# Attention weights of the third token group turned in 32 by 32 blocks on VectorE, with SBUF transfers on ScalarE's queue

## The chip, the cores and the metric

The kernel runs on 1 core of one Trainium2 chip. The metric is device time in microseconds of one launch; lower is better. The kernel before takes 2874.01 us (median of 3 runs, 2873.08 to 2874.37).

## The reference

One layer of a hybrid trunk is computed for a prompt of 2048 tokens and for 8 short samples of 16 tokens. One projection of the normalised input feeds three branches (a gated convolution, a gated linear recurrence and a stick-breaking attention) and the merge gates; the branches are projected, gated, added and projected again. The change lies in the attention of the prompt. Cut to that:

```python
def sb_attend(q, k, v, q_pos, k_pos):
    z = jnp.einsum('bqhd,bkhd->bhqk', qf, kf) * (1.0 / math.sqrt(SB_DH))
    causal = (k_pos[None, :] < q_pos[:, None])[None, None]
    log_1mb = jnp.where(causal, jax.nn.log_sigmoid(-z), 0.0)
    rest = lax.cumsum(log_1mb, axis=3, reverse=True) - log_1mb
    A = jnp.where(causal, jnp.exp(jax.nn.log_sigmoid(z) + rest), 0.0)
    return jnp.einsum('bhqk,bkhd->bqhd', A, vf)
...
h = rms_norm(x, norm_g[l])
(a_x, a_b, a_c, a_z, g_q, g_f, g_i, g_z,
 s_q, s_k, s_v, s_z, m_a, m_b, m_c) = split_cols(h @ w_in[l])
...
m = jax.nn.sigmoid(m_a) * y_a + jax.nn.sigmoid(m_b) * y_b + jax.nn.sigmoid(m_c) * y_c
return x + m @ w_out[l], ...
```

A weight A of query q and key k is sigmoid(z) times the product of sigmoid(-z) over the keys between them. There are 8 heads of 64 channels.

## The kernel before, in words

**Stages.** The 17 tiles of 128 tokens (one of samples, 16 of the prompt) go through the input projection in three token groups (`GROUPS`), each as a list of jobs: a job loads one piece of weights and multiplies it with two chunks of tokens (tile `acc`, lines 710 and 721). Every chunk of 3 tiles and 128 output channels takes 24 matmuls into one of two `acc` buffers, and ScalarE or VectorE empties the buffer afterwards (gates `gm` L1176, `hgz` L1135, `hgf` L1224 and others). After the third group comes the merge stage (lines 1440 and 1471), with three `acc` buffers.

**Background.** Attention and recurrence are generators. After every six `acc` matmuls the job loop gives them a credit in proportion to the work just written (`RATES`, `RATE_H`, `RATE_M`), and they write some of their instructions. Then a scheduler, which keeps the data dependences, sets the order on each engine. So the attention's matmuls stand among those of the jobs in TensorE's queue. Prompt attention begins with the third group (`open_attention`) and goes on through the merge stage.

**Attention.** Four blocks of 512 queries (`QBLOCKS`), each for four pairs of heads, each pair in segments of up to 512 keys. A segment is two steps (heads e = 0 and e = 1); a step is four turns, one for each tile i of 128 queries. One turn: two matmuls make the scores `z` in PSUM (two `z` buffers, which the recurrence uses too; L329, L330); ScalarE takes sigmoid(-z) into `snb` and sigmoid(z) into `sp` (L333, L335); VectorE forms the running product `pr` (L342) and multiplies it into `sp` (L347). The weights now stand with queries on the partitions, and the product with V needs keys there. So three turns later (`queue`, `DEPTH`) TensorE turns the turn's up to four blocks of 128 by 128 into PSUM tile `tp` (L310), and ScalarE copies it to `aT` (L311). When both heads of a segment are in `aT`, TensorE multiplies with V into `pv` (L359). After a pair's last segment, `store` multiplies by the gate `ot`, splits the result in two parts and stores them (L366, L182).

**Queues.** All transfers but a few gathers are issued by SyncE (SP), in the scheduler's order.

Of the kernel before, what the change touches and what calls it, by code (L numbers as in the profile page):

```python
# [8 lines left out]
F32 = mybir.dt.float32  # L9
# [7 lines left out]
P = 128  # L17
# [81 lines left out]
def trunk(ctx: ExitStack, tc: tile.TileContext, x_prompt, x_sample, cache_conv, state_hgrn, cache_k, cache_v,  # L99
# [3 lines left out]
    nc = tc.nc  # L103
# [137 lines left out]
    snb = []  # L241
    turn = [0]

    def open_attention():

        nonlocal at
        at = ctx.enter_context(tc.tile_pool(name="at", bufs=2, side="right"))

        for i in range(3):
# [18 lines left out]
    def load_step(m):  # L268
# [20 lines left out]
        if e == 0:  # L289
            Vt = at.tile([P, 4, 2, 64], F32, tag="Vt", name="Vt")  # L290
            nc.sync.dma_start(Vt[:, :nb], VV[(1 + b0) * P:(1 + b1) * P, h:h + 2].rearrange(
                "(b p) e c -> p b e c", p=P))
        else:
            Vt = held[m - 1][3]
        held[m] = (Q1, Q2, Kt, Vt)

    def attn_pair(m0, m1):
# [8 lines left out]
        def transposed(i, e, w, sp, aT):  # L306
# [4 lines left out]
            nc.scalar.copy(aT[:, e, 0:nb, i * P:(i + 1) * P], tp[:, :w].rearrange("p (b q) -> p b q", q=P))  # L311

        gate = []
        for m in range(m0, m1):
# [3 lines left out]
            if m == m1 - 1:  # L318
                gate.append(at.tile([P, 512], F32, tag="ot", name="ot", bufs=1))
                nc.sync.dma_start(gate[0][:, :n], SZ[pair][:, q0:q0 + n])  # L320
            Q1, Q2, Kt, Vt = held[m]
            nb = b1 - b0
            diag = si == 0
            if e == 0:
                aT = at.tile([P, 2, 4, 512], F32, tag="aT", name="aT", bufs=1)
            for i in range(nq):
# [22 lines left out]
                queue.append((True, lambda i=i, e=e, w=w, sp=sp, aT=aT: transposed(i, e, w, sp, aT)))  # L349
                yield from shorten(DEPTH)  # L350

            def accumulate(nb=nb, diag=diag, first=si == 0, last=last, Vt=Vt, aT=aT):
                if first:
                    box.append(ps_pv())
                pv = box[0]
                for j in range(nb):
                    c0 = j * P if diag else 0
                    for e in range(2):
                        nc.tensor.matmul(pv[64 * e:64 * e + 64, c0:n], Vt[:, j, e], aT[:, e, j, c0:n],  # L359
                                         start=first and j == 0, stop=last and j == nb - 1, skip_group_check=True)  # L360
            if e:
                queue.append((False, accumulate))
# [6 lines left out]
        queue.append((False, store))  # L369
# [11 lines left out]
    def attention(qi):  # L381
# [4 lines left out]
        yield from shorten(0)  # L386

# [1002 lines left out]
    tpools.close()  # L1390
    pst[0] = ctx.enter_context(tc.tile_pool(name="pst3", bufs=2, space=PSUM))
# [140 lines left out]
```

## Time and profile before

| | |
|---|---|
| median of 3 runs | 2874.01 us |
| profiled execution, its own time | 2876.11 us |
| its span, first to last instruction | 2873.2 us |
| prompt attention begins, by the first start of L329 | 1344.2 us |
| merge stage begins, by the first issue of `o` | 2176.8 us |
| granted TensorE clock | 1.00 |

The profile is one execution taken by the hardware profiler. PE is TensorE's matmuls, PEld its weight loads (they overlap), DVE VectorE, ACT ScalarE, POOL GpSimd, SP SyncE; q behind an engine's name is its instruction queue. Busy time is the union of the instructions' spans, and matmuls overlap each other, so a group's mean duration is longer than the time by which one matmul delays the next. "Releaser" is what ended an engine's idle time. Issuing a transfer isn't counted as busy on its engine, but the timeline shows how long it took there. The third token group with attention is nearly the stretch from 1341 to 2173 us, the merge stage the one from 2173 to 2873 us.

### The profile page before, as it was taken

To read this page: it belongs to the slowest core of one execution; us is meant where nothing else is said; L and a number is where in the kernel's file an instruction comes from. 1 tells how busy PE (TensorE), PEld (TensorE's weight loads), DVE (VectorE), ACT (ScalarE), POOL (GpSimd) and SP (SyncE) were. 2 spreads that over 40 slices of the span, in tenths; PEclk is the share of its full clock that TensorE was granted. 3 is DMA by queue.
4 is the path that set the end of the run, shared out by engine and by line. 5 is a ranking of instruction groups with operands and counts; after the bars stand their busy time and mean duration, and the time that the engine had idled before them with its cause. 6 is when DMAs were issued, how large, how long until landed. Compare 5 with 4: busy or idle time off the path is not lost.

```text
span 2873.2 us, 51723 instructions
## 1 busy us (share of the span) xinstructions
PE 2853.0 (99%) x19479; PEld 2662.3 (93%) x19479; DVE 1546.5 (54%) x3304; ACT 1018.7 (35%) x2375; POOL 331.8 (12%) x802
## 2 busy tenths in 40 slices
PE   9999999999999999999999999999999999999999
PEld 9999999999999999999999999999998888787888
DVE  5454635641344442545434747557485876867743
ACT  4333222242233332213334444434444444544420
POOL 3110000111200000001323111111010011010100
PEclk9999999999999999999999999999999999999999
DMA  8887777777678887746766454544447877878876
GB/s 306 305 276 247 231 241 244 231 243 243 212 249 266 276 265 243 243 167 192 237 215 202 146 173 136 173 139 151 144 145 238 286 234 239 266 250 266 271 250 210
DMA packets 370475, 649.76 MB, mean 226 GB/s; under 512 B 33481, under 2 KB 246306, under 8 KB 339506
## 3 DMA queue, kind: packets, MB, share of 16 engines
q1 hardware_dynamic: 369458, 644.36, 68.2%
q8 instruction: 154, 2.52, 0.4%
q0 software_dynamic: 768, 2.10, 0.2%
q14 instruction: 95, 0.78, 0.1%
HBM read 447.06 MB, written 199.27 MB: 225 GB/s over the span
## 4 chain that ended last, share of the span: by engine, by line
PE 76%; DVE 2%; DMA 2%; issue 1%; ACT 0%; POOL 0%; SPq 0%; DVEq 0%; POOLq 0%; ACTq 0%
PE acc L710 33%; PE acc L721 10%; PE acc L1440 9%; PE acc L1471 6%; PE pv L359 4%; PE tp L310 4%; PE z L330 2%; PE z L329 2%; PE z L1039 1%; PE tp L458 1%; DMA gate<-GM 1%; PE pv L522 1%; PE z L476 0%; PE hg L1086 0%; PE hg L826 0%
## 5 line engine op out<-in xcount | busy, mean ns | idle before, releaser
L710 PE MATMUL acc<-hx,w 128*128 128x384 f32 (+1 forms) x6816 | 1251.8, 333 | 0.1
L710 PEld LDWEIGHTS acc<-hx,w 128*128 128x128 f32 x6816 | 1106.5, 188 | 21.9 <-issue 15.2
L721 PE MATMUL acc<-w,hx 128*128 128x256 f32 x2544 | 328.6, 284 | 1.8 <-DVE hx L176 0.9
L342 DVE TENSOR_TENSOR_SCAN pr<-snb,carry 128x513 f32<-128x513 f32 x192 | 246.5, 1284 | 153.3 <-ACT snb L333 151.7
L721 PEld LDWEIGHTS acc<-w,hx 128*128 128x128 f32 x2544 | 310.9, 188 | 5.0 <-DVE hx L176 1.7
L311 ACT COPY aT<-tp 128x512 f32<-128x512 f32 (+2 forms) x320 | 167.6, 524 | 375.2 <-PE tp L310 361.3
L710 PE MATMUL acc<-hx,wst 128*128 128x384 f32 x1248 | 247.2, 344 | 0.0
L1440 PE MATMUL acc<-o,w 128*128 128x512 f32 (+2 forms) x1080 | 234.7, 363 | 1.8 <-DMA o<-OX 1.8
L333 ACT ACTIVATE snb<-z 128x512 f32<-128x512 f32 (+2 forms) x320 | 172.4, 539 | 144.5 <-PE z L330 140.4
L710 PEld LDWEIGHTS acc<-hx,wst 128*128 128x128 f32 x1248 | 215.4, 188 | 6.4 <-issue 3.7
L1440 PEld LDWEIGHTS acc<-o,w 128*128 128x128 f32 x1080 | 185.1, 188 | 33.8 <-issue 5.3
L347 DVE TENSOR_TENSOR sp<-sp,pr 128x512 f32<-128x512 f32 (+2 forms) x320 | 195.3, 611 | 29.2 <-POOL sp L338 3.7
L342 DVE TENSOR_TENSOR_SCAN pr<-snb,one 128x129 f32<-128x129 f32 (+3 forms) x128 | 114.4, 894 | 123.9 <-POOL snb L338 123.6
L310 PE MATMUL tp<-idf,sp 128*128 128x128 f32 x1088 | 171.3, 273 | 2.5 <-ACT aT L311 1.5
L335 ACT ACTIVATE sp<-z 128x512 f32<-128x512 f32 (+2 forms) x320 | 171.5, 536 | 0.0
L1471 PE MATMUL acc<-w,mh 128*128 128x256 f32 x816 | 161.2, 285 | 1.0 <-DVE yt L1479 0.8
L1176 ACT ACTIVATE gm<-acc 128x384 f32<-128x384 f32 (+1 forms) x144 | 68.2, 474 | 230.4 <-PE acc L710 197.5
L310 PEld LDWEIGHTS tp<-idf,sp 128*128 128x128 f32 x1088 | 131.8, 141 | 19.3 <-issue 4.4
L176 DVE TENSOR_TENSOR w<-wst,w 128x1024 fp32r<-128x1024 f32 x72 | 88.1, 1223 | 110.7 <-ACT w L175 107.9
L1471 PEld LDWEIGHTS acc<-w,mh 128*128 128x128 f32 x816 | 131.0, 188 | 7.2 <-issue 4.2
L329 PE MATMUL z<-Kt,Q 128*128 128x512 f32 (+2 forms) x320 | 128.8, 403 | 0.3 <-ACT sp L335 0.2
L359 PE MATMUL pv<-aT,Vt 128*64 128x512 f32 (+3 forms) x640 | 128.1, 535 | 0.0
(299 smaller groups left out, 3570.1 us busy)
## 6 DMA issues: line engine op xcount, KB each, us to landing
w<-W SPq DMA_DIRECT2D x168, 1024.0 KB, 6.0
W<-w SPq DMA_DIRECT2D x72, 1024.0 KB, 5.0
wst<-W SPq DMA_DIRECT2D x112, 512.0 KB, 5.1
wst<-in_w_in_dram SPq DMA_DIRECT2D x72, 512.0 KB, 5.1
GM<-gm SPq DMA_DIRECT2D x120, 192.0 KB, 3.7
W<-mwp SPq DMA_DIRECT2D x40, 512.0 KB, 4.2
Kt<-KT SPq DMA_DIRECT2D x160, 128.0 KB, 3.1
o<-OX SPq DMA_DIRECT2D x72, 256.0 KB, 4.7
```

Source lines behind the costliest of these rows:

```text
L310: nc.tensor.transpose(tp[:, j * P:(j + 1) * P], sp[:, j * P:(j + 1) * P], idf)
L311: nc.scalar.copy(aT[:, e, 0:nb, i * P:(i + 1) * P], tp[:, :w].rearrange("p (b q) -> p b q", q=P))
L329: nc.tensor.matmul(z[:, :w], Q1[:, i * P:(i + 1) * P], Kt[:, :w], start=True, stop=False)
L333: nc.scalar.activation(sn[:, 512 - w:512], z[:, :w], AF.Sigmoid, scale=-0.125)
L335: nc.scalar.activation(sp[:, :w], z[:, :w], AF.Sigmoid, scale=0.125)
L342: nc.vector.tensor_tensor_scan(pr[:, 512 - w:513][:, ::-1], s_in, s_in, one if diag else carry[e][i], ALU.mult, ALU.bypass)
L347: nc.vector.tensor_tensor(sp[:, :w], sp[:, :w], pr[:, 513 - w:513], ALU.mult)
L359: nc.tensor.matmul(pv[64 * e:64 * e + 64, c0:n], Vt[:, j, e], aT[:, e, j, c0:n], start=first and j == 0, stop=last and j == nb - 1, skip_g ...
L710: nc.tensor.matmul(acc[:, :n], w[0][a][:, k], hT[b][:, k, :n], start=k == 0 and i == 0, stop=k == KB - 1 and i == 2)
L721: nc.tensor.matmul(acc[:, :256], hT[b][:, k, ti * P:(ti + 1) * P], w[k // 4][a][:, k % 4], start=k == 0 and i == 0, stop=k == KB - 1 and i ...
L1440: nc.tensor.matmul(acc[:, :n], w[0][a][:, k, dd * P:(dd + 1) * P], box[x][b][:, k, sl], start=k == 0 and i == 0, stop=k == 3 and i == 2)
L1471: nc.tensor.matmul(acc[:, :256], box["l" if b else "h"][:, k, ti * P:(ti + 1) * P], w[k // 4][a][:, k % 4], start=k == 0 and i == 0, stop= ...
```

## The change

While the third token group runs (`by_blocks[0]` is true; it is set false behind that stage), a turn is no longer turned on TensorE. VectorE's transpose works inside 32 by 32 blocks: `turned_blocks` writes each turn's blocks to a tile `T`, and after the fourth turn of a step 16 transfers from SBUF to SBUF put the blocks in place in `aT`, one for each pair of a source quarter a and a destination quarter c of the partitions. All 16 are issued by ScalarE (`nc.scalar`). In the merge stage TensorE turns as before. `aT` has another layout, for both ways. The product with V of a segment and the store wait in `pending` until the next segment's second turn. `Vt` has one buffer and is loaded later, `snb` two in place of three, and `ot` and `oth` share the two buffers of `pr`.

```diff
+        turned_.append(at.tile([P, 4, 4, 4, 32], F32, name="T", bufs=1))
+        nc.gpsimd.memset(turned_[0], 0.0)
...
-            nc.scalar.copy(aT[:, e, 0:nb, i * P:(i + 1) * P], tp[:, :w].rearrange("p (b q) -> p b q", q=P))
+            nc.scalar.copy(aT[:, e, i, :, 0:nb], tp[:, :w].rearrange("p (b a q) -> p a b q", a=4, q=32))
+
+        def turned_blocks(i, e, w, sp, aT):
+
+            T = turned_[0]
+            nc.vector.transpose(T[:, i, :, 0:w // P].rearrange("p c b q -> p b c q"),
+                                sp[:, :w].rearrange("p (b c q) -> p b c q", c=4, q=32))
+            if i == nq - 1:
+                for a in range(4):
+                    for c in range(4):
+                        queue_ = nc.scalar
+                        queue_.dma_start(aT[32 * c:32 * c + 32, e, :, a], T[32 * a:32 * a + 32, :, c])
...
-                aT = at.tile([P, 2, 4, 512], F32, tag="aT", name="aT", bufs=1)
+                aT = at.tile([P, 2, 4, 4, 4, 32], F32, tag="aT", name="aT", bufs=1)
+                turn_ = turned_blocks if by_blocks[0] else transposed
...
+                if e == 0 and i == 1:
+
+                    queue.extend(pending)
+                    pending.clear()
+                if e == 1 and i == 2:
+                    Vt = at.tile([P, 4, 2, 64], F32, tag="Vt", name="Vt", bufs=1)
...
+                if last:
+                    gate.append(at.tile([P, 513], F32, tag="pr", name="ot", bufs=2))
...
-                        nc.tensor.matmul(pv[64 * e:64 * e + 64, c0:n], Vt[:, j, e], aT[:, e, j, c0:n],
+                        nc.tensor.matmul(pv[64 * e:64 * e + 64, c0:n], Vt[:, j, e],
+                                         aT[:, e, c0 // P:nq, :, j].rearrange("p i a q -> p (i a) q"),
...
-            th = at.tile([P, 512], F32, tag="oth", name="oth", bufs=1)
+            th = at.tile([P, 513], F32, tag="pr", name="oth", bufs=2)
```

By the built programs, 508 of TensorE's 1088 transposes of L310 and 160 of ScalarE's 320 copies of L311 go; 160 transposes on VectorE and 640 transfers on ScalarE's queue come. The 640 are 40 bursts of 16, each burst 1 MB in pieces of 64 KB (32 partitions, 4 rows of 512 bytes each).

Where the lists below come from the changed kernel, L341 and L342 are the scores (L329, L330 before), L345 and L347 the sigmoids (L333, L335), L739 the projection (L710), L382 the product with V (L359), L1164 and L1253 the gates (L1135, L1224).

ScalarE, before, in the third group, at the last `gz` job (the evacuations of `hgz`):

```order
L333 ACTIVATE snb_15449<-z 128x512
L335 ACTIVATE sp<-z 128x512
L1135 ACTIVATE hgz<-acc 128x384
L311 COPY aT<-tp 128x4x128
L333 ACTIVATE snb_15445<-z 128x512
L335 ACTIVATE sp<-z 128x512
L1135 ACTIVATE hgz<-acc 128x384
L311 COPY aT<-tp 128x4x128
```

ScalarE, now, at the same job; each row names the semaphores it waits for (DMAHW0 to DMAHW7 count the completions of transfers, of SP's and of ScalarE's alike; PE, DVE, Pool and Activation those engines' instructions). Seven more transfers follow on the last row:

```order
L1164 ACTIVATE hgz<-acc 128x384 [waits PE_49]
L345 ACTIVATE snb_15445<-z 128x512 [waits PE_49,Activation_49]
L347 ACTIVATE sp<-z 128x512 [waits DVE_49]
L322 DMA aT<-T 32x4x128 [waits DMAHW0_49,DVE_49]
L322 DMA aT<-T 32x4x128 [waits DMAHW1_49]
L322 DMA aT<-T 32x4x128 [waits DMAHW2_49]
L322 DMA aT<-T 32x4x128 [waits DMAHW3_49]
L322 DMA aT<-T 32x4x128 [waits DMAHW5_49]
L322 DMA aT<-T 32x4x128 [waits DMAHW7_49]
L322 DMA aT<-T 32x4x128 [waits DMAHW1_49]
L322 DMA aT<-T 32x4x128 [waits DMAHW2_49]
L322 DMA aT<-T 32x4x128 [waits DMAHW3_49]
```

The copies of `aT` between the sigmoids are gone, and all 16 transfers of a step stand in one piece between the sigmoids of two turns. The piece in one row, without the waits, and what stands behind it on ScalarE:

```order
L322 DMA aT<-T 32x4x128 x16
L345 ACTIVATE snb_15447<-z 128x512
L347 ACTIVATE sp<-z 128x512
L1164 ACTIVATE hgz<-acc 128x384
L345 ACTIVATE snb_15445<-z 128x512
L1253 ACTIVATE hgf<-acc 128x2x128
```

The next turn's two sigmoids, and the evacuations of two `acc` buffers, now stand behind the burst. Over the third group 15 of the 40 bursts stand in one piece like this, 19 have a piece of 10 to 15 transfers, and 6 are in pieces of 8 or fewer.

TensorE, before, around the second half of that `gz` job:

```order
L310 MATMUL tp<-idf,sp 128x128 x4
L710 MATMUL acc<-hx,w 128x384 x6
L329 MATMUL z<-Kt,Q_23200 128x512
L330 MATMUL z<-Kt,Q_23201 128x512
L710 MATMUL acc<-hx,w 128x384 x18
L310 MATMUL tp<-idf,sp 128x128 x4
```

TensorE, now, at the same job, from the scores whose sigmoids stand just ahead of the burst:

```order
L341 MATMUL z<-Kt,Q_23117 128x512
L342 MATMUL z<-Kt,Q_23118 128x512
L739 MATMUL acc<-hx,w 128x384 x18
L341 MATMUL z<-Kt,Q_23117 128x512
L342 MATMUL z<-Kt,Q_23118 128x512
L739 MATMUL acc<-hx,w 128x384 x6
L739 MATMUL acc<-hx,wst 128x384 x18
L341 MATMUL z<-Kt,Q_23393 128x512
L342 MATMUL z<-Kt,Q_23394 128x512
L739 MATMUL acc<-hx,wst 128x384 x6
L382 MATMUL pv<-aT,Vt 64x512
L341 MATMUL z<-Kt,Q_23393 128x512
```

The transposes are gone. Of the four score pairs that begin in this list, the second and the third stand behind the burst on ScalarE with their sigmoids; the last row needs the `z` buffer of the second, so the two sigmoids just behind the burst. The product with V right ahead of it is of the segment that the burst completes.

More of the change, by code (lines that the diff above doesn't have):

```diff
@@ L386, in attention @@
         yield from shorten(0)
+        if pending:
+            yield 5.0
+            queue.extend(pending)
+            pending.clear()
+            yield from shorten(0)
     def sample_attention():
```

33 lines of the change are left out of this document (17 added, 16 removed).

## The prediction

> **What bounds the kernel now.** I read the page first, for the busy shares and the chain that ended last.
>
> ```profile
> span 2873.2 us, 51723 instructions
> PE 2853.0 (99%) x19479; PEld 2662.3 (93%) x19479; DVE 1546.5 (54%) x3304; ACT 1018.7 (35%) x2375; POOL 331.8 (12%) x802
> PE 76%; DVE 2%; DMA 2%; issue 1%; ACT 0%; POOL 0%; SPq 0%; DVEq 0%; POOLq 0%; ACTq 0%
> ```
>
> TensorE is busy 99% of the span and holds 76% of the chain; no other engine has more than 2%. So TensorE's time is the time, as long as the others answer before it runs out of buffers. The windows of the two stages with attention come next (per window: us, then busy us of PE, PEld, DVE, ACT, POOL with counts, granted clock, DMA share, GB/s):
>
> ```profile
> 1341.00:2173.00 832.00, 828.73 (x5381) 776.79 (x5379) 480.56 (x1041) 333.45 (x837) 148.72 (x345) 1.00 0.53 170
> 2173.00:2873.00 700.00, 691.60 (x4334) 583.27 (x4333) 457.60 (x646) 267.74 (x536) 57.46 (x195) 1.00 0.77 254
> ```
>
> In the third group's 832 us TensorE idles 3.3. ScalarE is busy 333, issues no transfer, and answers in time. The clock is 1.00 throughout, so no term comes from it.
>
> **What goes.** The transposes' and the copies' own rows in the two windows (L310: PE, then PEld busy; L311: ACT busy), and TensorE's weight loads around one turn's four transposes:
>
> ```profile
> 1341.00:2173.00 832.00, 78.02 (x484) 59.80 (x484) 1.00 0.53 170
> 1341.00:2173.00 832.00, 76.25 (x154) 1.00 0.53 170
> 1799.72 0.53 PEld L310 LDWEIGHTS tp<-idf,sp 128*128 128x128 f32 x4
> 1800.22 1.01 PEld L710 LDWEIGHTS acc<-hx,w 128*128 128x128 f32 x6
> ```
>
> Four transposes move the next load back by 0.50 us, 0.125 each; the window's PEld time gives 59.80 / 484 = 0.124, its PE time 78.02 / 484 = 0.161, which overlaps its neighbours. I take 0.124: 508 x 0.124 = **63 us less work on TensorE** (82 by the other). It is all on the path. ScalarE loses 160 x 76.25 / 154 = 79 us, which nothing waited for.
>
> **What comes on VectorE.** No row shows its block transpose. Rows of this stage bound it for 512 columns: a product of two tiles takes 0.69, a scan 1.285 us.
>
> ```profile
> L342 DVE TENSOR_TENSOR_SCAN pr<-snb,carry 128x513 f32<-128x513 f32 x70 | 89.9, 1285 | 79.6 <-ACT snb L333 78.6
> L347 DVE TENSOR_TENSOR sp<-sp,pr 128x512 f32<-128x512 f32 x91 | 63.0, 692 | 8.6 <-POOL sp L338 2.6
> L333 ACT ACTIVATE snb<-z 128x512 f32<-128x512 f32 x93 | 55.9, 602 | 47.1 <-PE z L330 45.0 <-DVE sc L1040 1.4
> L335 ACT ACTIVATE sp<-z 128x512 f32<-128x512 f32 x92 | 55.0, 598 | 0.0
> ```
>
> I take the product's 0.69: 508 blocks are 127 tiles of 512 columns, 88 us (164 at the scan's). VectorE then has 480 + 88 = 569 us in 766 of TensorE's. The sum is hidden; without that cover the delay of one transpose is part of the chain below.
>
> **What comes on ScalarE.** It issues 640 transfers. There is no issue from ScalarE in the trace, so SP's rows must serve (start, us there, count):
>
> ```profile
> 1712.08 0.32 SPq L182 DMA_DIRECT2D OX<-oth  x1
> 2176.85 5.28 SPq L1410 DMA_DIRECT2D o<-OX  x8
> 2649.98 3.44 SPq L1410 DMA_DIRECT2D o<-OX  x7
> 693.71 4.54 SPq L529 DMA_DIRECT2D OCS<-od  x8
> 2644.98 0.59 SPq L281 DMA_DIRECT2D Q<-QT  x1
> 2645.62 0.59 SPq L282 DMA_DIRECT2D Q<-QT  x1
> ```
>
> One alone takes 0.32 us; back to back they take 0.49 (3.44 / 7), 0.57 (4.54 / 8), 0.64 (two starts of Q) and 0.66 (5.28 / 8). A burst is back to back: I take 0.6, so **16 x 0.6 = 9.6 us** (5.1 to 10.6) in which ScalarE evacuates nothing. It would then be taken for 333 - 79 + 40 x 9.6 = 638 us of 766, 83%, in blocks of nearly 10.
>
> What such transfers take until they land, and the queue's packets, in this window (KB each, median us; packets, MB, share of 16 engines):
>
> ```profile
> Kt<-KT SPq DMA_DIRECT2D x80, 128.0 KB, 2.8
> Vt<-VV SPq DMA_DIRECT2D x20, 256.0 KB, 2.9
> OX<-oth SPq DMA_DIRECT2D x10, 256.0 KB, 2.6
> OX<-ob SPq DMA_DIRECT2D x12, 128.0 KB, 1.7
> q1 hardware_dynamic: 74738, 139.69, 51.9%
> ```
>
> A rule of the Trainium skill speaks for a small block. "DMA: Bandwidth & Descriptors", section "Issuing engines are not separate DMA queues", says that the time in which a sequencer initiates a transfer is usually small beside the transfer. SP's rows disagree for small transfers: 0.59 us of issue for a Q piece, where a Kt piece of the same 128 KB lands after 2.8. By the rule the bursts would cost TensorE nothing, which is the first rival.
>
> **How long TensorE can go on.** Its own pace in this stage:
>
> ```profile
> 1801.52 0.48 PE L329 MATMUL z<-Kt,Q 128*128 128x512 f32 x1
> 1802.07 2.27 PE L710 MATMUL acc<-hx,w 128*128 128x384 f32 x12
> 1804.18 0.50 PE L1003 MATMUL z<-one,qk 128*128 128x1 f32 x4
> 1826.62 2.37 PE L359 MATMUL pv<-aT,Vt 128*64 128x512 f32 x16
> ```
>
> Twelve `acc` matmuls take 2.11 us from start to start, 0.176 each; a pair of scores 0.55. In the list shown for the last `gz` job, between the scores ahead of the burst and the row that needs a `z` buffer emptied behind it stand 18 + 6 + 18 + 6 matmuls, two pairs of scores and one product: 48 x 0.176 + 2 x 0.55 + 0.15 (2.37 / 16 in the run of products) = **9.7 us of cover**. On the other side: two sigmoids ahead of the burst 1.2 us, burst 9.6, two sigmoids 1.2, together 12.0. TensorE stands for 2.3 us. The product with V that follows waits for the burst's last transfer to land. SBUF to SBUF isn't in the trace; by the nearest rows (1.7 to 2.9 us) I take the store's 2.6. It lands at 1.2 + 15 x 0.6 + 2.6 = 12.8, against a cover of 10.4 at that row (9.7 + 0.55 + 0.15): 2.4 us, the same stand. Behind it the evacuations of two `acc` buffers are late too, and VectorE has a scan, a product and a transpose (2.7 us) waiting on the late `snb`; I add 0.6 for that and take 3 us for each of the 34 bursts with a piece of 10 or more, 1 us for the 6 in smaller pieces: 34 x 3 + 6 = **108 us that TensorE stands**.
>
> **The other edits.** The 640 transfers carry 42 MB, in 81,920 pieces of 512 bytes, beside 139.7 MB in 74,738 packets that take 51.9%. By bytes they add 16%, by packets 57%; the Vt rows (also 512 bytes, same landing as Kt's 2 KB) put it near the lower half. I charge nothing, hidden behind weights that are loaded a job ahead; at the upper end the DMA engines are full and weights come late, part of the second rival. The product with V now reads `aT` in runs of 32 elements. Neither this nor a slower read is in the trace; its bounds are 0 and twice its page row:
>
> ```profile
> L359 PE MATMUL pv<-aT,Vt 128*64 128x512 f32 (+3 forms) x640 | 128.1, 535 | 0.0
> ```
>
> that is, +128 us; I take 0, since the same matmul count and columns remain. `ot` and `oth` in `pr`'s buffers make VectorE's next scan wait for a store to land (2.6 us, 16 times, 42 us if nothing hid it); TensorE has `acc` work at these places, so 0. Two `snb` instead of three, the later Vt and the 2048-column memset on GpSimd (18% busy): 0, ScalarE mostly waits for TensorE there (47 us ahead of L333). The merge stage keeps its transposes: 0.
>
> **Sum.** 2876.1 (the profiled execution) - 63 + 108 = 2921; that execution is 2.1 us above the median, so **2919 us**, 1.6% slower. (Its span is 2.9 us shorter than its time.)
>
> **Rivals.**
> First, on the other side: **issue is cheap**. Place: ScalarE's bursts. At SP's single 0.32 us a burst takes 5.1; ScalarE is back after 1.2 + 5.1 + 1.2 = 7.5 us, within the cover of 9.7, the data land after 1.2 + 4.8 + 2.6 = 8.6, within 10.4. The point that decides is (9.7 - 2.4) / 16 = 0.46 us for each issue. For it: the single rows, and a run with 0.49, close by. Against it: 0.57 to 0.66. Time: 82 us gained, down to 63 with 25 us of stands left: 2794 to 2838, about 2820.
> Second, **the shared counters**. The list shows that a burst's seventh transfer waits for the counter of its second, and others for counters that SP's transfers use too. If every five transfers wait for one landing, a burst takes 16 / 5 x 2.6 = 8.3 us, less than its issue; but a transfer of SP's ahead on a counter (a weight piece lands in over 5 us, and SP itself waits for TensorE to free its buffer) holds ScalarE that much longer:
>
> ```profile
> w<-W SPq DMA_DIRECT2D x54, 1024.0 KB, 5.4
> SPq L208 <- PE acc L710: 131.0, 31, 12.3
> ```
>
> With 5.4 us more in most bursts the stand is 8 us: 34 x 8 - 63 = +209, 3085. Full DMA engines or a slow read of `aT` end there too, 3020 to 3120.
> Third, **it evens out**: the cover differs from place to place (the pieces of 10 to 15 leave ScalarE earlier by up to 3.6 us); with 1.5 us for each burst, 40 x 1.5 = 60 cancels the 63. That the transposes don't leave TensorE is excluded: the built program has 508 fewer.
>
> **Chances.** Forecast, 2885 to 2990: 0.50. Cheap issue: 0.28. Evens out, within 0.2% (about what a measurement of this kernel can tell from no change, 2868 to 2880): 0.08. Counters and the like, above 2990: 0.14. So faster 0.28, same 0.08, slower 0.64. For 8 in 10 I leave about 0.1 out on each side: 2822 to 3045. The likeliest case's own range is 2885 to 2990.
>
> **What would show it.** Right: in the third group's window TensorE's work about 63 us down and its idle time about 108 up, most of it released by ScalarE (`z` and `acc` evacuations) or by transfers to `aT`, once per burst; issues on ScalarE of about 0.6 us; the merge stage unchanged at 700 us. Wrong: issues near 0.3 us, or TensorE still at 99%; idle time put down to late weights; L382's duration above L359's 535 ns; or a merge stage that is longer.

## The result and the profile after

| | before | after |
|---|---|---|
| median (4 runs each, same chip) | 2874.19 us | 3113.83 us |
| lowest and highest | 2873.08, 2875.68 | 3104.64, 3121.29 |
| profiled execution, its own time | 2876.11 us | 3104.64 us |
| merge stage begins (first issue of `o`) | 2176.8 us | 2380.3 us |
| granted TensorE clock, mean | 1.00 | 0.966 |

The change makes the kernel slower: the ratio is 1.083, with a 95% interval of 1.080 to 1.087. The direction was forecast, the size was not: 2919 us was said, and even the upper end of the range, 3045, is too low.

The page of the changed kernel, in its order: span, busy times, the granted clock in 40 slices, the chain by engine and by line.

```profile
span 3102.8 us, 51494 instructions
PE 2905.4 (94%) x18971; PEld 2663.3 (86%) x18971; DVE 1608.9 (52%) x3463; ACT 939.5 (30%) x2215; POOL 337.7 (11%) x803
PEclk9999999999999999989999888898998999999999
PE 76%; DMA 12%; DVE 4%; ACTq 3%; issue 2%; ACT 1%; POOL 1%; SPq 0%; DVEq 0%; POOLq 0%
```

TensorE has 508 matmuls fewer and is busy *longer*, 2905.4 us against 2853.0. The clock row says most of why: from the 18th slice on, where the turning begins, there are eights. On the chain, transfers (12%) and ScalarE's own queue (3%) have come up. The windows of the two stages, cut at the first issue of `o`; the first two rows are of before, the next two of after:

```profile
1341.00:2176.80 835.80, 832.47 (x5402) 779.17 (x5400) 484.09 (x1045) 337.02 (x844) 149.09 (x347) 1.00 0.53 170
2176.80:2873.20 696.40, 687.85 (x4313) 580.89 (x4312) 454.07 (x642) 264.17 (x529) 57.09 (x193) 1.00 0.77 254
```
```profile
1341.00:2380.30 1039.30, 870.39 (x4869) 772.61 (x4869) 535.72 (x1188) 253.85 (x673) 147.50 (x341) 0.91 0.59 173
2380.30:3102.80 722.50, 702.71 (x4328) 588.38 (x4328) 464.18 (x658) 267.42 (x536) 63.31 (x197) 0.98 0.76 251
```

The third group takes 203.5 us more, the merge stage 26.1. In the third group TensorE idles 1039.3 - 870.4 = 168.9 us (before: 3.3), and its busy time is 37.9 us up though work was taken off it: the clock there is 0.91. Next, the triggers by their line (count: shortest/median/longest in ns, first and last start in us), and the longest of TensorE's waits in the third group (us in all, times, longest):

```profile
L322 ACTq DMA_DIRECT2D aT<-T x640: 592/612/1755, 1353.4 to 2452.9; - x160
DMA to landing us min/median/max: 2.0/3.7/9.1
```
```profile
PE z L341 <- ACT sp L347: 68.6, 17, 12.8
PE z L1068 <- ACT sp L347: 32.3, 8, 7.6
PE acc L750 <- ACT gm L1205: 11.9, 2, 7.0
```

An issue takes 0.612 us, as taken. TensorE waits for ScalarE to empty `z` and `acc` buffers. One burst, on ScalarE and then on TensorE (start, us, what; in brackets the idle time before and its releaser; the last row is the same product at the full clock, at another place of this kernel), and the granted clock behind the burst in windows of 2 us (TensorE's busy time, count, clock):

```profile
2174.77 0.49 ACT L1205 ACTIVATE gm<-acc 128x384 f32<-128x384 f32 x1
2175.14 12.12 ACTq L322 DMA_DIRECT2D aT<-T  x16
2187.36 0.60 ACT L345 ACTIVATE snb<-z 128x512 f32<-128x512 f32 x1 [12.10 <-DMA aT<-T]
```
```profile
2183.80 1.07 PE L382 MATMUL pv<-aT,Vt 128*64 128x512 f32 x2
2188.50 0.39 PE L341 MATMUL z<-Kt,Q 128*128 128x256 f32 x1 [3.63 <-ACT sp L347]
2189.34 4.88 PE L382 MATMUL pv<-aT,Vt 128*64 128x512 f32 x13
2018.45 3.65 PE L382 MATMUL pv<-aT,Vt 128*64 128x512 f32 x14
```
```profile
2188.00:2190.00 2.00, 1.49 (x6) 0.89 0.28 83
2190.00:2192.00 2.00, 2.00 (x8) 0.50 0.40 142
2192.00:2194.00 2.00, 2.00 (x7) 0.75 0.42 122
2194.00:2196.00 2.00, 2.00 (x10) 1.00 0.05 16
```

Sixteen triggers hold ScalarE for 12.1 us, 2.3 more than 16 x 0.612: their starts are 0.65 us apart, and twice in between ScalarE waits, 0.9 and 0.8 us, for an earlier transfer to end, once one of SP's. Over the run 13 bursts stand in one piece in the trace; they took 10.4 to 17.5 us, 13.3 on average. TensorE stands 3.6 us, and then works at half its clock for some 3.4 us: thirteen matmuls of the product with V (PV) in 4.88 us, where fourteen of the same width took 3.65 at the full clock. So a stand is paid for a second time. Added up over windows of 1 us from 1341 to 2460 (busy time times what the clock lacks of 1.00), the low clock costs 71.5 us, in 30 stretches; TensorE's timeline has 26 stands of 3 us and more there (25 up to the last trigger), together 142 us.

### The profile page after: what moved, and what is told of

It is laid out like the page before. It is cut to its first block, busy times and chain, and to the rows that moved or that the text cites. A ratio compares the mean times of both kernels' runs of the same rounds, so it can differ in the third digit from the quotient of the medians.

```text
span 3102.8 us, 51494 instructions
## 1 busy us (share of the span) xinstructions
PE 2905.4 (94%) x18971; PEld 2663.3 (86%) x18971; DVE 1608.9 (52%) x3463; ACT 939.5 (30%) x2215; POOL 337.7 (11%) x803
## 4 chain that ended last, share of the span: by engine, by line
PE 76%; DMA 12%; DVE 4%; ACTq 3%; issue 2%; ACT 1%; POOL 1%; SPq 0%; DVEq 0%; POOLq 0%
PE acc L739 34%; PE acc L750 11%; PE acc L1470 8%; DMA aT<-T 7%; PE acc L1501 6%; PE pv L382 4%; ACTq L322 3%; PE tp L310 2%; PE z L1068 2%; PE z L341 2%; PE z L342 2%; DVE pr L354 1%; DMA w<-W 1%; PE tp L487 1%; DVE T L316 1%
## 5 line engine op out<-in xcount | busy, mean ns | idle before, releaser
L739 PE MATMUL acc<-hx,w 128*128 128x384 f32 (+1 forms) x6816 | 1261.2, 336 | 17.5 <-ACT hgk L1255 7.2
L739 PEld LDWEIGHTS acc<-hx,w 128*128 128x128 f32 x6816 | 1125.5, 191 | 38.9 <-issue 12.8
L750 PE MATMUL acc<-w,hx 128*128 128x256 f32 x2544 | 335.5, 289 | 6.8 <-ACT gm L1205 4.9
L750 PEld LDWEIGHTS acc<-w,hx 128*128 128x128 f32 x2544 | 318.6, 193 | 12.4 <-ACT gm L1205 5.8
L345 ACT ACTIVATE snb<-z 128x512 f32<-128x512 f32 (+2 forms) x320 | 173.4, 542 | 475.1 <-DMA aT<-T 210.0
L739 PE MATMUL acc<-hx,wst 128*128 128x384 f32 x1248 | 250.6, 350 | 2.6 <-ACT gm L1205 1.8
L1470 PE MATMUL acc<-o,w 128*128 128x512 f32 (+2 forms) x1080 | 242.4, 370 | 10.1 <-DMA aT<-T 8.1
L739 PEld LDWEIGHTS acc<-hx,wst 128*128 128x128 f32 x1248 | 222.4, 193 | 11.4 <-issue 3.5
L359 DVE TENSOR_TENSOR sp<-sp,pr 128x512 f32<-128x512 f32 (+2 forms) x320 | 193.8, 607 | 55.1 <-POOL sp L350 26.3
L347 ACT ACTIVATE sp<-z 128x512 f32<-128x512 f32 (+2 forms) x320 | 171.7, 537 | 133.5 <-DVE T L316 67.0
L341 PE MATMUL z<-Kt,Q 128*128 128x512 f32 (+2 forms) x320 | 133.5, 418 | 74.9 <-ACT sp L347 74.2
L382 PE MATMUL pv<-aT,Vt 128*64 128x512 f32 (+3 forms) x640 | 161.6, 574 | 14.6 <-DMA aT<-T 11.1
L341 PEld LDWEIGHTS z<-Kt,Q 128*128 128x128 f32 x320 | 62.9, 197 | 93.7 <-ACT sp L347 86.4
L311 ACT COPY aT<-tp 128x512 f32<-128x512 f32 (+3 forms) x160 | 87.8, 551 | 171.6 <-PE tp L310 165.3
L382 PEld LDWEIGHTS pv<-aT,Vt 128*64 128x64 f32 x640 | 51.0, 144 | 87.6 <-issue 79.3
```

What stands on the lines that cost most here:

```text
L341: nc.tensor.matmul(z[:, :w], Q1[:, i * P:(i + 1) * P], Kt[:, :w], start=True, stop=False)
L345: nc.scalar.activation(sn[:, 512 - w:512], z[:, :w], AF.Sigmoid, scale=-0.125)
L347: nc.scalar.activation(sp[:, :w], z[:, :w], AF.Sigmoid, scale=0.125)
L359: nc.vector.tensor_tensor(sp[:, :w], sp[:, :w], pr[:, 513 - w:513], ALU.mult)
L739: nc.tensor.matmul(acc[:, :n], w[0][a][:, k], hT[b][:, k, :n], start=k == 0 and i == 0, stop=k == KB - 1 and i == 2)
L750: nc.tensor.matmul(acc[:, :256], hT[b][:, k, ti * P:(ti + 1) * P], w[k // 4][a][:, k % 4], start=k == 0 and i == 0, stop=k == KB - 1 and i ...
```

## The experiments

Theory A, ahead of the first: ScalarE, held in one piece by a burst, makes TensorE stand, and each longer stand lowers the clock. Theory B: the 42 MB of SBUF traffic do it, whoever issues them. Theory C: VectorE's transposes and their single tile `T` do. All edits are to the changed kernel unless it is said otherwise. Times are of one run each, beside the kernel before on the same chip (2874.1 to 2880.4 us over the runs, so differences under some 6 us mean nothing).

### Fewer triggers, the same bytes

```diff
+                nc.scalar.dma_start(aT[:, e], T)                    # e1_one, for the two loops
+                for c in range(4):                                  # e2_four
+                    nc.scalar.dma_start(aT[32 * c:32 * c + 32, e], T[32 * c:32 * c + 32])
```

> The 16 transfers of a burst become one transfer of the same 1 MB, still issued by ScalarE; the blocks are not put in their places, so this part of the turning is left out. Everything else is as in the changed kernel. Theory A (ScalarE is held in one piece by 16 issues and the waits among them, TensorE stands for it, and each stand costs a stretch at a low granted clock): one issue holds ScalarE about 0.6 us, the stands go, the clock of the third group is 1.00, and the time is 2800 to 2850 us (2876 less 63 us of transposes, plus little). Theory B (the bytes: 160 stores' worth of SBUF traffic delays the other loads or the matmuls' operands, whoever and however many issue it): the same 40 MB move, so the time stays above 2950 us and the clock below 0.95. Theory C (the VectorE transposes with their single tile T hold the chain up): nothing changes in them, so the time stays near 3100 us.

> Four transfers of 256 KB for the 16 of 64 KB, issued by ScalarE, the same bytes; as with one transfer the blocks are not put in their places. Theory A: four issues hold ScalarE about 2.4 us, less than the cover of TensorE, so the time is that of one transfer plus at most 20 us (2800 to 2870 us) with the clock at 0.99 or more in the third group. Theory B: above 2950 us, as with one. Theory C: near 3100 us.

Measured: **2868.8 and 2945.8 us** (before 2877.7). B falls, and so does C as it was put: with the same bytes, the same transposes and the same `T`, in one transfer, the kernel is no slower than before. But A missed both figures, the second by 76 us. With four triggers ScalarE's issue alone is small (160 x 0.515 = 82 us), but a transfer over 32 partitions takes long to land, and others wait for it. Who waited for the transfers (engine and line, us, times), first in e1_one, then in e2_four, and one burst of e2_four on ScalarE:

```profile
  DVE T L316: 52.3, 23
```
```profile
  ACT snb L343: 55.0, 8
  DVE T L316: 51.2, 20
  PEld pv L380: 22.8, 5
  PE pv L380: 22.3, 6
DMA to landing us min/median/max: 2.9/5.1/11.3
1799.66 7.98 ACTq L320 DMA_DIRECT2D aT<-T  x3
```

VectorE waits for `T` as long in the one as in the other, so that is not the difference. PV's waits are (2 us in e1_one), and ScalarE's: three triggers hold it for 8 us, because a trigger waits for an earlier transfer, and in all its 160 triggers hold it for 168 us, twice their issue. So a second thing came in: transfers that land late, waited for by the next triggers and by PV.

### The same triggers from other queues

```diff
-                        queue_ = nc.scalar
+                        queue_ = nc.sync                            # e3_sp
+                        queue_ = nc.sync if c % 2 else nc.scalar    # e4_alt
+                        queue_ = nc.gpsimd                          # e10_pool
```

> All 16 transfers of a burst as in the changed kernel, same shapes and bytes, issued by SP instead of ScalarE. Theory A: ScalarE is free, so its sigmoids follow at once; what is late next is SP's own loads behind a burst (weights, Kt, Vt, the next step's Q), 10 to 14 us each time. Time 2820 to 2950 us, the clock of the third group 0.97 or more; if SP's loads have a turn's lead, near 2830. Theory B: no better than the changed kernel by more than 50 us (3050 to 3115 us), since the same transfers run. Theory C: near 3100 us.

> The 16 transfers of a burst dealt out in turn to ScalarE and SP, eight each. Theory A: ScalarE is held about 8 x 0.61 = 4.9 us and some waits, 5 to 8 us in one piece, less than the 9.7 us that the prediction took as cover: most stands go, those left are shorter than 3 us, the clock is 0.97 or more in the third group, and the time is 2820 to 2920 us. If the loss were in proportion to the issues on ScalarE and not a matter of one piece against a cover, half of the loss would stay: 2960 to 2980 us. Theory B: 3050 to 3115 us.

> All 16 transfers of the changed kernel, same shapes, issued by GpSimd, which is busy 11% of the time. Theory A: nothing that TensorE needs at once stands behind GpSimd's triggers but the carry copies and the small chains; ScalarE and SP are free. 2840 to 2900 us if a trigger costs GpSimd no more than 0.6 us; 2900 to 3000 us if it costs 1 us and more, since then pv and the next transposes wait for aT and T (16 us and more per burst). The bytes as such (rival): 2960 us and more, as 128 us go with them.

Measured: **3032.6, 2911.4 and 2993.5 us**. The mixed one lies in A's range: with eight triggers each on ScalarE and SP the loss against before is 34 us instead of 229. All on SP is slower than A said: SP's triggers stand in line with its loads, so VectorE waits for `T` (first row) and TensorE for weights, and the clock of the third group is 0.95 all the same. GpSimd takes 0.548 us for a trigger, but its triggers wait up to 17.1 us for what comes ahead of them (third row), so `T` and `aT` are late; the time lies 93 us above the range that A gave for triggers of no more than 0.6 us, and meets the one for triggers of 1 us and more, whose reason it has (late `T` and `aT`) but not its condition. It meets B's figure too, but B had fallen with the single transfer.

```profile
  DVE T L316: 97.1, 15
PE acc L739 <- DMA w<-W: 18.2, 6, 6.6
L322 POOLq EVENT_SEMAPHORE  x110: 17/43/17142, 1380.7 to 2309.9; - x110
```

### Each part alone

```diff
-            nc.vector.transpose(T[:, i, :, 0:w // P].rearrange("p c b q -> p b c q"),
+            nc.vector.transpose(aT[:, e, i, :, 0:w // P].rearrange("p c b q -> p b c q"),   # e5_direct
-                        queue_.dma_start(aT[32 * c:32 * c + 32, e, :, a], T[32 * a:32 * a + 32, :, c])
+                        nc.scalar.dma_start(                        # e6_tiny: e5_direct and these 16
+                            T[32 * c:32 * c + 32, 2 * e, a, 0, 0:8], aT[32 * a:32 * a + 32, e, i, c, 0, 0:8])
-    by_blocks = [True]                                              # e7_noturn
+    by_blocks = [False]
```

> VectorE turns the 32 by 32 blocks as in the changed kernel, but writes them straight into aT, and no transfer runs: putting the blocks in their places is left out. One transfer of 1 MB took 2868.8 us, some 55 us above 2876 less the 63 us of the transposes. If those 55 us belong to the transfers (landing of 5.8 us, the wait for T): 2805 to 2830 us. If they belong to the VectorE transposes or to the other edits: 2855 to 2875 us.

> As without transfers, but ScalarE issues 16 transfers of 1 KB each after a burst's last transpose, into a spare place: the same number of issues and of waits for a transfer's end as in the changed kernel, and almost no bytes; putting the blocks in their places is left out. Theory A (issues and the waits among them hold ScalarE): 3000 to 3110 us, idle of TensorE in the third group over 110 us, its granted clock there 0.95 or less. Theory B (the bytes): under 2900 us. If the issues count but the waits between them come from the bytes' landing: bursts of some 10 us instead of 13, and 2930 to 3000 us.

> The other edits of the change alone: TensorE's transposes and ScalarE's copies stay in the third group too, with two snb tiles instead of three, Vt loaded late into one buffer, ot and oth in pr's buffers, and the PV product reading the new layout of aT. If these cost nothing, as the prediction took: 2870 to 2886 us (before: 2877.7 on the chip of the first runs). If they are behind the 12 us that the merge stage is longer in every run so far, or behind a part of the 55 us: 2890 to 2930 us.

Measured: **2836.8, 2976.7 and 2876.7 us** (before 2880.4). The third group's windows, in this order (e5, e6, e7):

```profile
1341.00:2137.90 796.90, 786.63 (x4890) 724.16 (x4890) 538.28 (x1189) 265.47 (x678) 139.57 (x343) 1.00 0.55 177
```
```profile
1341.00:2268.90 927.90, 837.02 (x4897) 749.34 (x4896) 537.29 (x1189) 254.37 (x676) 155.00 (x343) 0.96 0.49 154
```
```profile
1341.00:2180.30 839.30, 832.83 (x5401) 778.70 (x5399) 483.89 (x1045) 336.89 (x844) 148.64 (x347) 1.00 0.53 169
```

The other edits cost nothing; of the holding back of PV in `pending` e7 says nothing, since it doesn't have it. From e7 to e5 the turning moves to VectorE, and `pending` comes in: 832.83 - 786.63 = 46.2 us less on TensorE, 0.091 for each of 508 transposes, and 40 us less time; VectorE's 93 us are hidden. From e5 to e6 only the triggers come, with 1/64 of the bytes: **+140 us**. This is A's mechanism by itself, though the time is below A's 3000, the idle time is 90.9 us, not 110, and the clock is 0.96, where 0.95 or less was said. The time lies in the range of the third case, in which the waits between the triggers come from the landing: the nine bursts in one piece took 10.4 to 11.9 us here, against 13.3 on average in the changed kernel.

### The clock after a stand

```diff
+        for k, count in enumerate((1, 3, 4, 5, 6, 7, 8, 10, 14, 24, 0)):   # e8_clock: before, and this at its end
...
+                    nc.tensor.matmul(pt, wt, rhs, start=x == 0, stop=x == 9)   # 100 in all
+            nc.scalar.copy(t, pt)
+            for x in range(count):
+                nc.scalar.mul(t, t, 0.5)
+            rhs = sb.tile([P, 512], F32R, name=f"rhs{k + 1}")
+            nc.scalar.copy(rhs, t)
```

> The kernel before, and behind its end a separate stretch: eleven batches of 100 matmuls of 128x512, each but the first waiting for a chain of ScalarE operations on the batch before it (1, 3, 4, 5, 6, 7, 8, 10, 14, 24 operations and two copies), so that TensorE stands for some 2, 3, 3.5, 4, 4.5, 5, 6, 7, 9 and 15 us. Theory A: behind a stand under some 3 us the clock stays 1.00; behind each longer one the first 3 to 6 us of the batch run at 0.50, the same stretch for every length, so each such stand costs about 2 to 3 us beside its own length. Rival: the clock does not follow from stands (it stays 1.00 in all batches), or it falls more the longer the stand.

Measured: the batches' rows in TensorE's timeline (six of the eleven; start, duration of 100 matmuls, and in brackets the stand before them), and the clock behind the stands of 1.99, 3.31 and 17.19 us:

```profile
2900.16 22.97 PE L1531 MATMUL probe<-rhs,wt 128*128 128x512 f32 x100 [1.99 <-ACT rhs L1537]
2926.43 24.32 PE L1531 MATMUL probe<-rhs,wt 128*128 128x512 f32 x100 [3.31 <-ACT rhs L1537]
2954.72 25.44 PE L1531 MATMUL probe<-rhs,wt 128*128 128x512 f32 x100 [3.97 <-ACT rhs L1537]
2984.79 25.72 PE L1531 MATMUL probe<-rhs,wt 128*128 128x512 f32 x100 [4.63 <-ACT rhs L1537]
3147.78 24.52 PE L1531 MATMUL probe<-rhs,wt 128*128 128x512 f32 x100 [10.58 <-ACT rhs L1537]
3189.49 25.81 PE L1531 MATMUL probe<-rhs,wt 128*128 128x512 f32 x100 [17.19 <-ACT rhs L1537]
```
```profile
2900.16:2902.16 2.00, 2.00 (x9) 1.00 0.03 8
2926.43:2928.43 2.00, 2.00 (x5) 0.50 0.00 0
2928.43:2930.43 2.00, 2.00 (x9) 0.78 0.00 0
3189.49:3191.49 2.00, 2.00 (x5) 0.50 0.03 8
3193.49:3195.49 2.00, 2.00 (x6) 0.50 0.00 0
3195.49:3197.49 2.00, 2.00 (x10) 0.99 0.00 0
```

The stand of 2.0 us costs itself alone. From 3.3 us on the batch is 1.4 to 2.8 us longer, and the price does not grow with the stand (1.6 us behind 10.58): half the clock for some 3 to 6 us. So the low clock *follows from* the stands, here with next to no transfer beside them. The Trainium skill, "TensorE: Matmul & The Clock Gate", section "Why this matters for your kernels", advises against gaps of over some 3 us for this reason; these rows agree.

But 3 us is no sharp limit, and one stand of 2 us proves little. In e1_one, which has no stand of 3 us, the clock falls five times; one of them, the stand's row and the window behind it:

```profile
1373.93 2.84 PE L747 MATMUL acc<-w,hx 128*128 128x256 f32 x12 [2.03 <-ACT kn L840]
1374.00:1376.00 2.00, 2.00 (x10) 0.51 0.77 291
```

Counted over 15 traces, of the changed kernel and 14 of its variants (1341 to 2470 us, single stands: no other of 0.5 us or more within 7 us before or 3.5 us behind), the clock is low behind 1 of 72 stands of 1.0 to 1.5 us, 9 of 35 up to 2.0, 14 of 28 up to 2.5, 16 of 19 up to 3.0, 21 of 23 up to 3.5, and behind all 87 longer ones.

### How the bytes cost what they cost

From 1 KB transfers (2976.7) to the changed kernel (3104.6) there are 128 us. Two candidates: the pieces that a transfer consists of, and who waits for its end.

```diff
-queue_.dma_start(aT[32 * c:32 * c + 32, e, :, a], T[32 * a:32 * a + 32, :, c])
+queue_.dma_start(aT[32 * c:32 * c + 32, e, a], T[32 * a:32 * a + 32, c])   # e9_runs: T and aT laid out for it
+nc.scalar.dma_start(T[32 * c:32 * c + 32, :, a], aT[32 * a:32 * a + 32, e, :, c])   # e13_bytes: e6_tiny, 64 KB each
-                                         aT[:, e, c0 // P:nq, :, j].rearrange("p i a q -> p (i a) q"),
+                                         strided(turned_[1], 0, [0, nq - c0 // P], [1, P]) if blk else   # e18_pvfree
+                                         aT[:, e, c0 // P:nq, :, j].rearrange("p i a q -> p (i a) q"),
```

> All 16 transfers on ScalarE as in the changed kernel, the whole computation, but T and aT are laid out so that each transfer moves one unbroken run of 2 KB per partition instead of four of 512 bytes. Same issues, same bytes, a quarter of the pieces. With transfers of 1 KB the 16 issues alone gave 2977 us and the changed kernel 3105, so 128 us come with the bytes. If they come by the transfers' slow ends (3.7 us to landing, waited for in the next triggers and by pv): landing falls to 2 to 2.5 us, the time to 2980 to 3050 us. If they come by the bytes as such: 3080 to 3115 us.

> VectorE turns straight into aT, and ScalarE issues the 16 transfers of 64 KB the other way, from aT into T: same issues, same bytes as in the changed kernel, but neither pv nor the transposes read what a transfer brings (a transpose into aT still waits until the transfers have read it); putting the blocks in their places is left out. With 1 KB each the same order took 2976.7 us, the changed kernel 3105. If the 128 us are the bytes' doing through ScalarE (a trigger waits for an earlier transfer's end, and these take longer to land): 3060 to 3110 us, ScalarE held some 540 us for its triggers as in the changed kernel (461 with 1 KB). If they are the wait of pv and of the transposes for landed data: 2975 to 3010 us.

> The changed kernel with all its transposes and transfers, but in the third group the PV product reads a constant tile instead of aT (same matmuls, same columns), so it waits for no transfer, and no transfer waits for it; the PV product's operand is what is left out. With the transfers turned round (nothing waits for what they bring, the transposes write two halves in turn) 3009 us, the changed kernel 3105: 96 us are still open. If pv's wait for landed data and the triggers' wait for pv are these 96 us: 3005 to 3030 us. If they are the single T, which the next transposes can't write before the transfers have read it, and ScalarE's order behind it: 3085 to 3110 us. Between: both, in proportion.

Measured: **3095.7, 3009.4 and 3106.2 us**. Longer runs change nothing, neither the landing (3.6 us median, not the 2 to 2.5 that were expected) nor much of the time. Turned round, the same bytes cost 33 us over 1 KB, though ScalarE is held as long as in the changed kernel (the rows of its queue add up to 534 us against 541, with 1 KB to 443). So the other 95 us come with what this run leaves out, the waits of PV and of the transposes for the data. PV alone is hardly it: freed of `aT`, it leaves the time where it was. That run isn't quite clean, since PV, now earlier, ran into the late load of `Vt` instead:

```profile
PE z L343 <- ACT sp L349: 59.2, 17, 10.5
PE z L1071 <- ACT sp L349: 30.6, 7, 6.2
PE pv L384 <- DMA Vt<-VV: 27.6, 6, 10.8
```

These 27.6 us may hide a gain; the two rows above them are nearly those of the changed kernel (68.6 and 32.3). That leaves the single `T`, or `T` and PV together: in e13 the transposes write two halves in turn, in the changed kernel one tile. This is an argument by elimination, and no run has the one without the other. VectorE's rows ahead of the burst at 2175.14, and its whole wait for `T` in the changed kernel (us, times):

```profile
2170.14 0.71 DVE L316 STREAM_TRANSPOSE T<-sp 128x512 f32<-128x512 f32 x1 [1.67 <-DMA aT<-T]
2171.72 0.68 DVE L316 STREAM_TRANSPOSE T<-sp 128x512 f32<-128x512 f32 x1
2173.50 0.68 DVE L316 STREAM_TRANSPOSE T<-sp 128x512 f32<-128x512 f32 x1
2174.41 0.69 DVE L316 STREAM_TRANSPOSE T<-sp 128x512 f32<-128x512 f32 x1
  DVE T L316: 25.0, 11
```

The first waits until the last burst's transfers have read `T`; all four then run within 5 us, and the next burst follows at once, in one piece. So here burst, landing, four transposes and the next burst are one closed chain. But VectorE waits for `T` only 11 times, 25.0 us in all, and e1_one, with twice that (52.3 us), is only 32 us slower than e5_direct, which has no such wait. Where the 95 us come from therefore stays open. SBUF has no room for a second `T` beside the rest, so there is no run with two.

### Cutting the bursts, and versions to beat both

```diff
+                def place(c):                                       # e14_quarters
+                    for a in range(4):
+                        nc.scalar.dma_start(aT[32 * c:32 * c + 32, e, :, a], T[32 * a:32 * a + 32, :, c])
+                place(0)
+                queue[0:0] = [(False, lambda c=c: place(c)) for c in range(1, 4)]
+                yield 1.7 * w / 512 - (0.45 if by_blocks[0] else 0.0)   # e16_paced: with this
```

e11_runsalt is e9_runs with the queues of e4_alt; e12_three deals four triggers to ScalarE, four to SP, eight to GpSimd; e15_quartalt and e17_pacedalt are e14_quarters and e16_paced with runs of 2 KB and every second trigger on SP.

> The changed kernel with each burst cut in four: four triggers behind the last transpose, the other twelve as three items of four in the queue of later turns, so that sigmoids come between; all on ScalarE, same count, same shapes. Theory A (what counts is the length of a piece against the cover, and the clock follows from stands over some 3 us): pieces of 4 to 6 triggers, 3 to 5 us, few stands over 3 us, granted clock in the third group 0.97 or more, 2900 to 2980 us. If the loss goes by the number of issues on ScalarE, in whatever pieces: 3070 to 3115 us. If the later end of a burst makes pv and the next transposes late instead: also above 3050 us, but with the waits at pv and T and not at the sigmoids.

> Both remedies together: bursts cut in four, half of the triggers on SP, runs of 2 KB. Theory A: pieces of two on ScalarE, 1.2 us each, SP's loads held up by 1.2 us at a time: 2860 to 2895 us (one burst in one go over the two queues: 2910). If it stays at 2900 us or above, what is left is not the pieces but the transfers' landing, waited for by T and pv.

> Bursts cut in four on ScalarE as before, but the time that the added items take in the plan is taken off elsewhere, so that all 40 bursts (640 triggers) stay in the third group; in the run before this one only 32 were there, the rest was turned on TensorE in the merge stage, so its 3012 us doesn't compare. Theory A (length of a piece against the cover): fewer stands over 3 us than the 25 of the changed kernel, 2980 to 3050 us. By number alone: 3090 to 3115 us.

> Runs of 2 KB, and the 16 transfers dealt out to ScalarE and SP in turn. With runs of 512 bytes that gave 2911 us (before: 2877.7 on that chip). If the shorter landing shortens the waits: 2875 to 2900 us; if the eight issues alone are what is left: 2900 to 2915 us.

> Runs of 2 KB, four transfers of a burst on ScalarE, four on SP, eight on GpSimd. The floor is the run with no transfer at all, 2837 us, and the run with one transfer of 1 MB, 2869. Theory A: ScalarE and SP are held 2.4 us each, under the cover, no stand over 3 us: 2845 to 2885 us, so 0.987 to 1.003 of the time before. If GpSimd's triggers or its part in VectorE's port hold the chain up: 2890 to 2950 us.

> The same with half of the triggers on SP and runs of 2 KB, all 40 bursts in the third group. With 32 bursts it gave 2889 us. Theory A: pieces of two or three triggers on ScalarE: 2870 to 2905 us, 0.997 to 1.010 of the time before; no version with the transfers is then faster than the kernel before by more than 0.3%.

Measured: 3012.2 and 2889.2 us, but with 32 of the 40 bursts (the transpose's count is 128, not 160; the rest was turned on TensorE in the merge stage), so these two don't compare. With all forty, **3072.8** (e16), **2910.0** (e11), **2914.8** (e12, ratio 1.014, 1.012 to 1.016) and **2920.3** (e17, 1.016, 1.014 to 1.018). The last two miss A's ranges by 30 and 15 us (e12 lies in the range of its rival, that GpSimd's triggers hold the chain up), and no version that puts the blocks in place is faster than before. Cutting gains only 32 us of the 229, between what A said (2980 to 3050) and what the number alone would give: ScalarE's rows show 30 pieces of seven triggers and more even then (35 in the changed kernel), since it has little else to put between. So it stays open whether the length of a piece counts, or all the time that ScalarE is held. Beside each other (triggers on ScalarE for each burst; idle time of TensorE in the third group; what the low clock costs, summed as above):

| run | us | triggers | idle, us | stands of 3 us and more | low clock, us |
|---|---|---|---|---|---|
| after | 3104.6 | 16 | 168.9 | 26 | 71.5 |
| e9_runs | 3095.7 | 16 | 167.1 | 26 | 62.1 |
| e16_paced | 3072.8 | 16, cut | 148.4 | 19 | 49.9 |
| e3_sp | 3032.6 | 0, 16 on SP | 104.2 | 7 | 46.9 |
| e13_bytes | 3009.4 | 16, turned round | 114.6 | 13 | 44.7 |
| e6_tiny | 2976.7 | 16, 1 KB | 90.9 | 8 | 30.7 |
| e2_four | 2945.8 | 4 | 62.5 | 7 | 29.0 |
| e12_three | 2914.8 | 4, 8 on GpSimd | 61.8 | 5 | 13.5 |
| e11_runsalt | 2910.0 | 8 | 43.0 | 3 | 11.1 |
| e1_one | 2868.8 | 1 | 26.7 | 0 | 8.1 |
| e5_direct | 2836.8 | 0 | 10.3 | 0 | 1.6 |

Time, idle time and low clock go much together, whoever issues; the number of triggers on ScalarE alone does not order the rows (e2_four has four, e11_runsalt eight). With all sixteen on ScalarE, its work (254 us) and the triggers (508 of their 541 us lie here) fill nearly three quarters of the third group; with eight there and eight on SP (259 and 213 us) little over half, and far more than half of the loss is gone.

## Why the prediction was wrong

Its direction held, and so did the core of its mechanism: triggers on ScalarE make TensorE stand (e6). Four terms of its sum didn't. The profiled execution is 184 us above the sum's 2921: 64 are the low clock in the third group, 58 longer stands, 17 a smaller saving, 26 the merge stage, and some 20 are left.

- **The step that failed: "The clock is 1.00 throughout, so no term comes from it."** That was so of the kernel before, which has no long stand there. The forecast itself put 34 stands of 3 us into the sum, and then charged the low clock behind them at nothing. It cost 71.5 us, 64 of them in the third group; e8 shows that it follows from stands alone.
- **"34 x 3 + 6 = 108 us that TensorE stands"** was mis-sized: idle time rose by 168.9 - 3.3 = 165.6 us in the third group. There were fewer stands of 3 us and more, 26, but of 5.5 us each (142 / 26). One cause is shown: a burst in one piece took 13.3 us on average, not 9.6, since the issues start 0.65 us apart and waits for earlier transfers come between them. That the single `T` bound the bursts to one another is argued, not shown. (The 0.15 us of a product in the cover is a mean over 128 to 512 columns; 512 take 0.23 to 0.26. That moves next to nothing.)
- **Landing taken as 2.6 us** measured 3.7 at the median, 9.1 at most. What waits for it was named as PV alone. The sum had neither the waits of later triggers (33 us from 1 KB to 64 KB, by e13) nor those of the next transposes for `T` (25.0 us on VectorE; what they cost the kernel is open).
- **-63 us** was mis-sized: e7 to e5 gives 46.2. The measure 0.124 came from the time of the weight loads; a transpose was worth 0.091 here, and why it is less no run shows.
- **"The merge stage keeps its transposes: 0"**: it was 26.1 us longer, of which 11.2 are idle time (19.8 against 8.6) and 7.6 low clock. The last bursts run into it, to 2452.9 us; without transfers (e5, e7) it has 697.2 and 694.7 us, as before.

For the third group: -46 + 166 of idle time + 64 of low clock (71.5 less what lies past 2380) = +184, measured +203.5. The other 20 us are in time that the profile counts as busy, and some 15 of them in PV, whose matmuls take 84.7 us of TensorE's time there against 56.1 in e5_direct, about 13 of it by the low clock:

```profile
1853.74 3.65 PE L359 MATMUL pv<-aT,Vt 128*64 128x512 f32 x16
```

That is a whole product of before, sixteen matmuls. In the changed kernel they are broken up: in 19 places two stand alone (as at 2183.80, 1.07 us), and where fourteen are left, these take 3.65 us as well (the row at 2018.45).

Right were: the issue of 0.6 us (0.612), with which the rival of a cheap issue falls; VectorE's 88 us (93.0 measured), hidden; PV's reading of runs of 32 elements, and `snb`, `Vt`, `ot`, `oth` at nothing (e7); a DMA traffic that by itself brings little (e1). The second rival, waits for earlier transfers between the triggers, was a part of it rather than another way: +33 us of the 128 from 1 KB to 64 KB (e13), and much of e2_four. Its 3020 to 3120 us hold the measured time, but in part by luck: its stands of 8 us come to 272 us, where 166 of idle time were measured and the low clock, which it didn't have either, brought 64 more. Its 14% were too few, as the range was built of cases that added no clock.

## What to carry to other kernels

Where a forecast has TensorE stand for 3 us or more, add some 2 us of low clock for each stand, and ask whether the same wait could be broken into stands of under 1.5 us; between 1.5 and 3 us the clock fell in part of the cases. Count triggers as work of the engine that issues them (0.6 us each here) with the waits among them, up to 8 us for three triggers in e2_four: here ScalarE, which empties PSUM for a busy TensorE, could not give three quarters of its time away, and half of the triggers did far less than half of the harm. A single staging tile between an engine and a burst of transfers ties each burst to the reading of the last; a forecast should have that wait, though no run here shows what it costs.

## What the runs showed of the hardware

- The clock falls to 0.50 behind every stand of 3.5 us and more (87 of 87), behind half of those of 2.0 to 2.5 us (14 of 28), and hardly ever behind 1.0 to 1.5 us (1 of 72). The price does not grow on with the stand: in e8 1.4 us behind 3.31, 2.8 us behind 4.63, 1.6 behind 10.58, 2.8 behind 17.19.
- The issue does not grow with the size: a median of 0.612 us for 64 KB in runs of 512 bytes, 0.601 in runs of 2 KB and also for 1 KB, 0.515 for 256 KB, 0.472 for 1 MB over 128 partitions.
- A transfer of 1 MB over 128 partitions lands after 5.8 us in the median, one of 256 KB over 32 partitions after 5.1, one of 64 KB over 32 partitions after 3.7 in bursts from ScalarE and 2.0 from SP alone.
- The sixteen PV matmuls of a segment take 3.65 us at 512 columns; broken into two and fourteen, they take 1.07 and 3.65 us.
- VectorE turns 128x512 fp32 in 32 by 32 blocks in 0.696 us (94 of them: 65.0 us), the time of its product of two tiles (0.692).
